# Whole-row first conditioning, head group pairs in sequence, and cached keys spread over the new keys' tiles

## The chip, the cores and the metric

The kernel runs on one core of a Trainium2 chip. The metric is device time in microseconds (us) of one execution; less is better. The core has five engines that each run their own instructions in order: TensorE (PE, with its weight loads PEld), VectorE (DVE), ScalarE (ACT), GpSimd (POOL) and SyncE (SP), which here issues nearly all DMAs.

## The reference

It is one inference step of a two layer encoder over 1024 prompt rows and 32 sample rows of width 1024, all in float32. Layer 0 mixes with an mLSTM, layer 1 with chunk-band attention; each is followed by an MLP.

```
for l in (0, 1):
    sh1, sc1, g1, sh2, sc2, g2 = split(silu(c) @ w_ada[l] + b_ada[l], 6)
    u = x * (1 + sc1) + sh1
    if l == 0:                                  # mLSTM
        q|k, v, o, gates = split(u @ w_in)      # q, k through a causal convolution
        y = (head_norm(mlstm_scan(q, k, v, gates)) * sigmoid(o)) @ w_out
    else:                                       # chunk-band attention
        kv = (x * (1 + kv_scale) + kv_shift) @ w_kv        # one K/V, 4 kv heads
        # 16 heads; a chunk of 64 queries sees its own and the 8 chunks before it;
        # the sample's rows see 512 cached keys and their own 32
        y = softmax(q @ k.T / 8 + bias) @ v @ w_out
    x = layer_norm(alpha * x + (1 + g1) * y)
    u = x * (1 + sc2) + sh2
    x = layer_norm(alpha * x + (1 + g2) * (square(relu(u @ w_up)) @ w_down))
```

The conditioning vector c differs between prompt and sample rows. The outputs are the last x of both, and the new states and K/V rows.

## The kernel before

Every product of full precision is made of three matmuls on a high and a low half (`proj`, lines 118 to 120, and the v steps at 455 to 457): high by high, high by low, low by high. Weights arrive in a `raw` tile and are split into halves of a `wc` tile, the high one by an ACT cast (L89), the low one by a DVE subtraction (L90); `wtile` does both. The pool `ring` has 3 slots for `raw` and 6 for `wc`; a slot is used again when its last reader is done. The 1056 rows are cut into three blocks `TBS`: 384, 384 and 288.

A work list, `Flow`, holds generators with due times. The main loops call `flow.tick()`, and a generator that is due puts its next instructions in there; `finish` puts in what is left. A scheduler then orders each engine's instructions, except for PE in the attention, whose order is kept as written.

The places that the change touches, in order of time:

**The start.** `ada_start(half)` (L386) makes the first conditioning (shift and scale of layer 0) in two halves. Each half takes, for each of 8 chunks of c, two blocks of 128 x 512 of `w_ada` (256 KB) through tiles that rotate over several tags, and adds into two groups of 32 PSUM partitions (`ada`, L392). The sums are copied to `sada` (L399), transposed (L401) and the bias is added (L403). Half 0 gives chunks 0 to 3 of the modulation: then the first four chunks of the v projection of head 0 (`v_proj`, `first_half`) run for three row tiles, while half 1 is loaded. `x_block` (L367) transposes x chunk by chunk into PSUM (L375), modulates it from there (`modulate`: ACT L324, DVE L326 and L329) into `U`, high and low, and copies it to `xt` (ACT, L380), from which it is written to DRAM (`xsp`) for the residual. A v tile is 8 chunks of 3 matmuls. Behind v_0 come the q and k projections (`qk`) and the recurrences.

**Keys and values.** Four tiles of cached keys are split (`kd_c`, ACT L1135, DVE L1136) and transposed (`kt_c`, PE L1141, in `put_keys`) one after another; then comes a loop over nine tiles of new rows, each with 48 matmuls against `wkv`.

**Attention.** `att_group(gp, c, e)` is one chunk c (16 is the sample) of one kv head, 2 gp + e: scores `s` (PE, L1234), bias and row maximum `mx` (DVE, L1245), exponential (ACT, L1248), transposition of `p` (`pt`, L1264) to `pT`, and the value product `pv` (L1284), whose result is split in place into `QO`. A list alternates wide and slim chunks, and takes gp 0 and gp 1 of a chunk next to each other. The bias rows lie in four `wc` tiles (bias0 to bias3) throughout.

**The junction.** After attention `open_acc(1, fwd)` loads the residual's three blocks (`acc<-xsp`, L808), `gain_shift` (ACT, L893) scales them, 24 instructions, and `out_proj` (L962) runs the output projection `op_b` in two groups of column pairs, (0,) and (1, 2, 3), over the blocks 2, 1, 0. `wo_block` loads and casts its weights (`w_ob`) when a group begins.

**The norm of layer 1.** `norm` is a generator: sums, then after `w[0]` ticks a mean (`mean_n`), then after `w[1]` ticks a variance (`var_n`, both PE, L842), then the modulated input `u` of the MLP. For the first norm of layer 1 the delays are `W10`, and a tick is worth 4 or 3 for each projected tile. Before a block's first `up` matmuls its norm is finished.

Of the kernel before, what the change touches and what calls it, by code (L numbers as in the profile page):

```python
# [15 lines left out]
P = 128  # L16
# [59 lines left out]
def trunk_kernel(ctx: ExitStack, tc: tile.TileContext, a, o):  # L76
# [120 lines left out]
    PRE = 3  # L197
    pre = {(k, q): ada_load(k, q, wc_tile) for k, q in ((0, 0), (0, 2), (1, 0), (1, 2))[:PRE]}
    c_rows = raw_tile([16, P], "c_rows")
    nc.sync.dma_start(c_rows[0:8], a["c_prompt"].rearrange("b (k p) -> (b k) p", p=P))  # L200
    nc.sync.dma_start(c_rows[8:16], a["c_sample"].rearrange("b (k p) -> (b k) p", p=P))
    tp = tpt("tp_c")
# [13 lines left out]
    rows2 = raw_tile([NPT2, P], "rows2")  # L216
    nc.sync.dma_start(rows2[0:96], a["b_ada"].rearrange("l (k p) -> (l k) p", p=P))
    nc.sync.dma_start(rows2[96:112], a["b_ada_kv"].rearrange("(k p) -> k p", p=P))
# [112 lines left out]
    START = 5  # L331
# [18 lines left out]
    def rot(fs):  # L350
        seq = [f for f, n in fs for _ in range(n)]
        cnt = [0]

        def f(shape, name):
            cnt[0] += 1
            return seq[cnt[0] % len(seq)](shape, name)
        return f

# [8 lines left out]
    def x_block(t0, n, load=True):  # L367
        if load:
            x_load(t0, n)
        for k in range(KC):  # L370
            ps = tpt(f"xps_{t0}_{k}")
            for i in range(0, n, P):
                xr = xrows[t0, i]
                m = xr.shape[0]
                nc.tensor.transpose(ps[:, i:i + m], xr[:, k * P:(k + 1) * P], ident[:m, :m])  # L375
# [4 lines left out]
            nc.scalar.copy(xt[:, k, t0:t0 + n], ps[:, :n])  # L380
            yield
        nc.sync.dma_start(xsp[0][:, :, t0:t0 + n], xt[:, :, t0:t0 + n])

    start_tile = rot([(raw_tile, 3), (wc_tile, 4), (y_tile, 1), (rc_tile, 1)])

    def ada_start(half):  # L386

        ps = adat(f"ada_0{half}")
        for k in range(KC):
            for q in (half, half + 2):  # L390
                raw = pre.pop((k, q), None) or ada_load(k, q, start_tile)
                nc.tensor.matmul(ps[32 * q:32 * q + 32, :512], cs[:, k, :], raw[:, :512],  # L392
                                 start=(k == 0), stop=(k == KC - 1))
            yield
        sb = rc_tile([P, 512], f"sada_0{half}")
        ps2 = nmt(f"adat_0{half}")
        for i, q in enumerate((half, half + 2)):
            rows = slice(32 * q, 32 * q + 32)
            (nc.scalar.copy if i else nc.vector.tensor_copy)(sb[rows], ps[rows, :512])  # L399
            for b in range(4):  # L400
                nc.tensor.transpose(ps2[:, i * P + b * 32:i * P + b * 32 + 32], sb[rows, b * P:(b + 1) * P],  # L401
                                    ident[rows, rows])
            nc.vector.tensor_tensor(  # L403
                ada[:, 4 * q:4 * q + 4, :], ps2[:, i * P:(i + 1) * P].rearrange("p (b j) -> p b j", b=4)[:, :, 0:2],
                pt2[:, 4 * q:4 * q + 4][:, :, None].broadcast_to([P, 4, 2]), op=ALU.add)
        ap = ada[:, KC + 4 * half:KC + 4 * half + 4, :]
        nc.vector.tensor_scalar_add(ap, ap, 1.0)

    ag = flow.add(ada_start(0))
    for i in range(START):  # L410
        flow.tick()
    x_load(*TBS[0])
    flow.finish(ag)
    xg = [x_block(t0, n, t0 == TBS[2][0]) for t0, n in TBS]


# [20 lines left out]
    def v_proj(h, after, first=None):  # L437
        ncols = 264 if h == 0 else 256

        def srcs(r0):  # L440
            def f(raw):
                r = [(raw[:, :, 0:256],
                      w_in[r0:r0 + 512, 1024 + h * 256:1024 + (h + 1) * 256].rearrange("(k p) c -> p k c", p=P))]
                if h == 0:
                    r.append((raw[:, :, 256:264], w_in[r0:r0 + 512, 3072:3080].rearrange("(k p) c -> p k c", p=P)))
                return r
            return f
        ws = [wtile(f"v{h}_0", srcs(0), ncols)]
        vts = []

        def part(ps, t, ks):
            for k in ks:
                w = ws[k // 4]
                uh, ul = uap(0, k, t * P, P), uap(1, k, t * P, P)
                nc.tensor.matmul(ps[:, :ncols], uh, w[:, 0, k % 4, :], start=(k == 0), stop=False)
                nc.tensor.matmul(ps[:, :ncols], uh, w[:, 1, k % 4, :], start=False, stop=False)
                nc.tensor.matmul(ps[:, :ncols], ul, w[:, 0, k % 4, :], start=False, stop=(k == KC - 1))
        begun, between = first(part) if first else ([], None)
        ws.append(wtile(f"v{h}_1", srcs(512), ncols, between=between))
        for t in range(NT):  # L460
            m = P if t < NT - 1 else TS
            if t < len(begun):
                ps = begun[t]
                part(ps, t, range(4, KC))
            else:
                ps = mmt(f"v_{h}_{t}")
                part(ps, t, range(KC))
            vt = A.tile([P, 258], F32, tag="vt", name=f"vt_{h}_{t}", bufs=9)
            nc.scalar.copy(vt[:m, :256], ps[:m, :256])
            nc.gpsimd.memset(vt[:m, 256:258], 1.0)  # L470
            if h == 0:
                nc.vector.tensor_copy(bass.AP(g64.tensor, g64[:m, t, 0:4].offset, [g64[:m].ap[0], [32, 2], [1, 4]]),
                                      ps[:m, 256:264].rearrange("p (a b) -> p a b", a=2))
            vts.append(vt)
            after(t)
        return vts
# [220 lines left out]
    xa = [None, None, xg[2]]  # L697

    def after_v0(t):
        flow.tick()  # L700
        if t == 2:
            flow.finish(xa[1])
            flow.add(xa[2])
        elif t == 5:
            flow.finish(xa[2])
    def first_half(part):

        ag = flow.add(ada_start(1))
        for _ in range(4):
            next(xg[0])  # L710
            flow.tick()
        begun = []
        for t in range(TBS[0][1] // P):
            begun.append(mmt(f"v_0_{t}"))
            part(begun[t], t, range(4))
            flow.tick()
        flow.finish(ag)

        def rest():
            x_load(*TBS[1], wc_tile)  # L720
            for _ in xg[0]:
                pass
            xa[1] = flow.add(xg[1])
            flow.add(small_params(), SP)
        return begun, rest
    vts = [v_proj(0, after_v0, first_half)]
# [89 lines left out]
    W10 = (8.0, 8.0, 0.0, 0.0, 0.0, 3.0)  # L816
# [355 lines left out]
    for t in range(4):  # L1172
        cr = tmp_t([P, 256], f"ck_{t}")
        nc.sync.dma_start(cr, ck[t * P:(t + 1) * P])
        flow.add(put_keys(cr, P, TP + t * P, f"c{t}"))
        flow.tick()
# [140 lines left out]
    pts = {}  # L1317

    wide = [(gp, c) for c in (8, 12, 13, 14, 15, 9, 10, 11) for gp in range(2)]
    slim = [(gp, c) for c in (7, 6, 5, 4, 16, 3, 2, 1, 0) for gp in range(2)]  # L1320
    units = []
    for i in range(18):
        units += wide[i:i + 1] + slim[i:i + 1]
    with tc.manual_schedule(engines={mybir.EngineType.PE}):
        for gp, c in units:
            for e in range(2):
                flow.add(att_group(gp, c, e))
                flow.tick()
# [6 lines left out]
    accs_cm, acc = open_acc(1, fwd)  # L1335
# [13 lines left out]
    wo = a["w_out_b"][0]  # L1349

    def wo_block(pr, half):
        cols = wo[:, 256 * pr:256 * pr + 256]
# [81 lines left out]
```

## Time and profile before

| | us |
|---|---|
| median of 3 runs | 2532.17 (2531.4 to 2533.92) |
| profiled execution | 2531.46 |
| span of its profile | 2529.6 |
| PE busy | 2466.1 (97%) |
| DVE busy | 1677.0 (66%) |
| ACT busy | 953.2 (38%) |
| POOL busy | 165.8 (7%) |
| bytes moved by DMA | 201.20 MB, 80 GB/s on average |

The profile has busy times by engine, a chain that ended last (followed back from the last instruction), waits by releaser, windows with the clock that the throttle granted to PE, and a timeline. A line such as `PE op_b L118 <- ACT w_ob L89: 6.4, 2, 5.0` says that PE waited at line 118 for the tile w_ob of ACT's line 89, 6.4 us over 2 times, the longest 5.0. A timeline line starts with the start and the duration, names engine, line, operation, the tile written and the tiles read, and ends with the idle time before it and what ended that. Consecutive matmuls overlap in these records, so a matmul's cost in a stream is the distance between two starts.

### The profile page before, as it was taken

How to read it: one execution, taken by the hardware profiler on the slowest of the kernel's cores; microseconds unless marked ns; L12 is line 12 of the kernel's file. 1: busy time of each engine (PE TensorE's matmuls, PEld its weight loads, DVE VectorE, ACT ScalarE, POOL GpSimd, SP SyncE). 2: the span in 40 equal slices, each digit the busy share in tenths (PEclk: the TensorE clock that was granted, in tenths of full speed). 3: DMA queues.
4: the chain of work that ended last, by engine and by line, in shares of the span. 5: the costliest groups of instructions: out<-in, count | busy, mean ns of one | idle time of the engine just before them, and what ended most of it. 6: DMA issues, size and time to landing. Idle time of an engine off the chain costs nothing.

```text
span 2529.6 us, 39897 instructions
## 1 busy us (share of the span) xinstructions
PE 2466.1 (97%) x15784; PEld 2356.0 (93%) x15784; DVE 1677.0 (66%) x3851; ACT 953.2 (38%) x2023; POOL 165.8 (7%) x315
## 2 busy tenths in 40 slices
PE   7999999999999999999999899989999999999998
PEld 3899999999999999999999877689999999999997
DVE  3899998788678678766597677737634334343337
ACT  3654446383212211221376566637621221221222
POOL 0111100000000000000001144400000000000003
PEclk9999999999999999999999999989999999999999
DMA  7522323413224234223123400051111111111101
GB/s 235 166 89 92 95 80 105 152 34 102 90 85 136 81 94 132 87 90 122 59 84 102 101 1 1 6 156 34 51 51 42 51 43 50 42 59 34 51 26 70
DMA packets 192063, 201.20 MB, mean 80 GB/s; under 512 B 9336, under 2 KB 180748, under 8 KB 191876
## 3 DMA queue, kind: packets, MB, share of 16 engines
q1 hardware_dynamic: 191876, 198.65, 25.4%
q8 instruction: 124, 2.03, 0.3%
q14 instruction: 63, 0.52, 0.1%
HBM read 183.38 MB, written 17.60 MB: 79 GB/s over the span
## 4 chain that ended last, share of the span: by engine, by line
PE 83%; DVE 7%; ACT 3%; DMA 3%; issue 1%; SPq 0%; DVEq 0%; POOL 0%; ACTq 0%
PE dn L118 10%; PE dn L120 10%; PE dn L119 10%; PE up L118 10%; PE up L119 9%; PE up L120 9%; PE pv L1284 2%; PE pt L1264 2%; PE s L1234 2%; DVE ada_room L236 1%; PE q L118 1%; PE q L119 1%; PE q L120 1%; DMA ada_room<-in_w_ada_dram 1%; PE op_a L118 1%; PE op_a L119 1%
## 5 line engine op out<-in xcount | busy, mean ns | idle before, releaser
L118 PE MATMUL dn<-h,w_dn 128*128 128x384 f32 (+2 forms) x1568 | 505.9, 323 | 0.0
L120 PE MATMUL dn<-h,w_dn 128*128 128x384 f32 (+2 forms) x1568 | 502.1, 320 | 0.0
L119 PE MATMUL dn<-h,w_dn 128*128 128x384 f32 (+2 forms) x1568 | 497.8, 317 | 0.0
L959 DVE SCALAR_TENSOR_TENSOR acc<-dn,ada,acc 128x384 f32<-128x384 f32 (+5 forms) x536 | 244.0, 476 | 237.2 <-PE dn L120 235.0
L118 PEld LDWEIGHTS dn<-h,w_dn 128*128 128x128 f32 x1568 | 294.5, 188 | 0.8 <-issue 0.2
L119 PEld LDWEIGHTS dn<-h,w_dn 128*128 128x128 f32 x1568 | 294.3, 188 | 0.1
L120 PEld LDWEIGHTS dn<-h,w_dn 128*128 128x128 f32 x1568 | 294.0, 187 | 0.0
L998 DVE TENSOR_TENSOR r<-r 128x384 f32<-128x384 f32 (+1 forms) x192 | 100.0, 523 | 275.6 <-ACT h L997 275.0
L996 ACT ACTIVATE r<-up 128x384 f32<-128x384 f32 (+1 forms) x192 | 88.5, 462 | 448.0 <-PE up L120 437.2
L118 PE MATMUL up<-U,w_up 128*128 128x384 f32 (+1 forms) x768 | 249.3, 325 | 0.0
L119 PE MATMUL up<-U,w_up 128*128 128x384 f32 (+1 forms) x768 | 248.2, 323 | 0.0
L120 PE MATMUL up<-U,w_up 128*128 128x384 f32 (+1 forms) x768 | 247.4, 322 | 0.0
L118 PE MATMUL up<-u,w_up 128*128 128x384 f32 (+1 forms) x768 | 246.5, 321 | 0.0
L120 PE MATMUL up<-u,w_up 128*128 128x384 f32 (+1 forms) x768 | 246.5, 321 | 0.0
L119 PE MATMUL up<-u,w_up 128*128 128x384 f32 (+1 forms) x768 | 246.4, 321 | 0.0
L89 ACT CAST w_up<-raw_up 128x1024 fp32r<-128x1024 f32 x64 | 66.8, 1048 | 413.1 <-PE dn L120 274.3
L236 DVE SCALAR_TENSOR_TENSOR aacc<-rada,cs,aacc 128x256 f32<-128x256 f32 x448 | 190.4, 478 | 0.0
L118 PEld LDWEIGHTS up<-U,w_up 128*128 128x128 f32 x768 | 144.2, 188 | 0.1
L120 PEld LDWEIGHTS up<-U,w_up 128*128 128x128 f32 x768 | 144.3, 188 | 0.0
L120 PEld LDWEIGHTS up<-u,w_up 128*128 128x128 f32 x768 | 144.2, 188 | 0.0
L119 PEld LDWEIGHTS up<-U,w_up 128*128 128x128 f32 x768 | 144.2, 188 | 0.0
L119 PEld LDWEIGHTS up<-u,w_up 128*128 128x128 f32 x768 | 144.1, 188 | 0.0
(318 smaller groups left out, 5260.5 us busy)
## 6 DMA issues: line engine op xcount, KB each, us to landing
raw_up<-in_w_up_dram SPq DMA_DIRECT2D x64, 512.0 KB
raw_dn<-in_w_down_dram SPq DMA_DIRECT2D x64, 512.0 KB
rada<-in_w_ada_dram SPq DMA_DIRECT2D x48, 512.0 KB
ada_room<-in_w_ada_dram SPq DMA_DIRECT2D x32, 512.0 KB
rada<-in_w_ada_dram SPq DMA_DIRECT2D x32, 256.0 KB
rada<-in_w_ada_kv_dram SPq DMA_DIRECT2D x16, 512.0 KB
acc<-xsp SPq DMA_DIRECT2D x4, 1536.0 KB
rc<-rc_d SPq DMA_DIRECT2D x8, 528.0 KB
```

Of the source, the lines that this page charges most:

```text
L89: nc.scalar.copy(dst_h, src)
L118: nc.tensor.matmul(ps, wh, mov(0, k), start=(k == 0), stop=False)
L119: nc.tensor.matmul(ps, wh, mov(1, k), start=False, stop=False)
L120: nc.tensor.matmul(ps, wl, mov(0, k), start=False, stop=(k == nk - 1))
L236: nc.vector.scalar_tensor_tensor(acc[:, cnd], raw[:, k], sc, acc[:, cnd], op0=ALU.mult, op1=ALU.add)
L959: nc.vector.scalar_tensor_tensor(xs, ps[:, off + o:off + o + mm_], gate[:, fc, cnd:cnd + 1], xs, op0=ALU.mult, op1=ALU.add)
L996: nc.scalar.activation(r, ps[:, :n], AF.Relu)
L998: nc.vector.tensor_mul(r, r, r)
L1234: nc.tensor.matmul(s[:, b, :w], qst, kk[i][:, g, k0 + j0:k0 + j0 + w], start=(i == 0), stop=(i == 1))
L1264: nc.tensor.transpose(pt[:kp, j - j0, pr * P:(pr + 1) * P], ps_[pr][:, j * P:j * P + kp], ident)
L1284: nc.tensor.matmul(pv[64 * e:64 * e + 64, :nq], V[:kp, vt0 + j, g * 64:(g + 1) * 64], pts[e][:kp, j, :nq], start=(j == 0), stop=(j == nt - 1))
```

## The change

Four things are changed together.

1. **Start.** `ada_load(k)` loads a whole row block of `w_ada`, 128 x 2048, as two DMAs of 512 KB into one `wc` tile; `c_rows` and the bias rows are loaded ahead of them. On SP's queue follow rows 0 to 3, x block 0, rows 4 and 5, half of the v weights, rows 6 and 7, the other half, x blocks 1 and 2. `ada_mm(k)` adds four products into four groups of 32 partitions, and `ada_first` transposes once for all; the 1 of 1 + scale is added to the bias beforehand. x is transposed to `xt` first (`x_transpose`) and modulated from there (`u_chunks`). v of head 0 (`v_first`) runs block by block and, within a block, chunk by chunk over three tiles; between chunks stand the transposes and the modulation of the next block. The writes to `xsp` stand behind v.
2. **Cached keys.** `cached_keys(t)` becomes a generator on the work list, started at the new tiles 0, 2, 4 and 6.
3. **Attention and output projection.** All 17 chunks of gp 0 come before those of gp 1. In gp 1, after units 8 and 11, the two halves of the first output projection weight are loaded and cast in `wc` slots of bias tiles that no later unit reads. `open_acc` loads the blocks in the order in which they are used (2, 1, 0), with the weight pairs 1 and 2 between them.
4. **Norm delays.** `W10` begins with 10, 12 instead of 8, 8.

The diff, without removed helpers:

```
-    def ada_load(k, q, mk):
-        raw = mk([P, 512], f"rada_0_{k}_{q}")
-        nc.sync.dma_start(raw, a["w_ada"][0, k * P:(k + 1) * P, q * 512:(q + 1) * 512])
+    def ada_load(k):
+        raw = wc_tile([P, 2 * D], f"rada_0_{k}")
+        for i in range(2):
+            nc.sync.dma_start(raw[:, i * D:(i + 1) * D], a["w_ada"][0, k * P:(k + 1) * P, i * D:(i + 1) * D])
         return raw
...
+    adaw = [ada_load(k) for k in range(4)]
...
+    nc.vector.tensor_scalar_add(pt2[:, KC:2 * KC], pt2[:, KC:2 * KC], 1.0)
...
+    def x_transpose(t0, n, eng):
+        for k in range(KC):
+            ps = tpt(f"xps_{t0}_{k}")
...
+            eng[k % len(eng)](xt[:, k, t0:t0 + n], ps[:, :n])
+            yield
+    def u_chunks(t0, n):
+        for k in range(KC):
             for off, m, cnd in segs(t0, n):
                 tmp = A.tile([P, 384], F32, tag="tmp", name=f"utmp_{t0}_{k}_{off}", bufs=3)
-                modulate(ps[:, off:off + m], m, sc1[:, k, cnd:cnd + 1], sh1[:, k, cnd:cnd + 1],
+                modulate(xt[:, k, t0 + off:t0 + off + m], m, sc1[:, k, cnd:cnd + 1], sh1[:, k, cnd:cnd + 1],
                          uap(0, k, t0 + off, m), uap(1, k, t0 + off, m), tmp[:, :m])
             yield
+    def ada_mm(k):
+        for q in range(4):
+            nc.tensor.matmul(ada_ps[32 * q:32 * q + 32, :512], cs[:, k, :], adaw[k][:, q * 512:(q + 1) * 512],
+                             start=(k == 0), stop=(k == KC - 1))
+    def ada_first():
+        sb = rc_tile([P, 512], "sada")
+        ps2 = nmt("adat")
+        for hf in range(2):
+            (nc.scalar.copy if hf else nc.vector.tensor_copy)(sb[:, 256 * hf:256 * hf + 256],
+                                                              ada_ps[:, 256 * hf:256 * hf + 256])
+            for b in (2 * hf, 2 * hf + 1):
+                nc.tensor.transpose(ps2[:, b * P:(b + 1) * P], sb[:, b * P:(b + 1) * P], ident)
...
+    def v_first(ws, nxt):
+        vts = []
+        for bi, (t0, n) in enumerate(TBS):
+            ts = range(t0 // P, (t0 + n + P - 1) // P)
+            pss = {t: (mmt, nmt, mmt)[bi % 2 * (t % 2)](f"v_0_{t}") for t in ts}
+            for k in range(KC):
+                for t in ts:
+                    v_chunk(pss[t], ws, t, k)
+                nxt(bi, k)
+            vts += [v_out(pss[t], 0, t) for t in ts]
         return vts
...
+    xT = [x_transpose(t0, n, (nc.scalar.copy, nc.vector.tensor_copy)[:2 - (i > 0)]) for i, (t0, n) in enumerate(TBS)]
+    uT = [u_chunks(t0, n) for t0, n in TBS]
+    x_load(*TBS[0])
+    adaw += [ada_load(k) for k in (4, 5)]
+    for k in range(4):
+        ada_mm(k)
+    vw = [v_weight(0, 0)]
+    adaw += [ada_load(k) for k in (6, 7)]
+    for k in range(4, 6):
+        ada_mm(k)
+    for _ in xT[0]:
+        pass
+    for k in range(6, 8):
+        ada_mm(k)
+    vw.append(v_weight(0, 1))
+    x_load(*TBS[1], wc_tile)
+    x_load(*TBS[2])
+    ada_first()
+    for _ in uT[0]:
+        pass
+    flow.add(small_params(), SP)
...
+    vts = [v_first(vw, next_u)]
+    for t0, n in TBS:
+        nc.sync.dma_start(xsp[0][:, :, t0:t0 + n], xt[:, :, t0:t0 + n])
...
-    def open_acc(l, order):
+    def open_acc(l, order, between=None):
...
-        for ti in order:
+        for ti in order if between is None else reversed(order):
             t0, n = TBS[ti]
             nc.sync.dma_start(accs[ti], xsp[l][:, :, t0:t0 + n])
+            if between:
+                between(ti)
...
-    W10 = (8.0, 8.0, 0.0, 0.0, 0.0, 3.0)
+    W10 = (10.0, 12.0, 0.0, 0.0, 0.0, 3.0)
...
-    for t in range(4):
+    def cached_keys(t):
         cr = tmp_t([P, 256], f"ck_{t}")
         nc.sync.dma_start(cr, ck[t * P:(t + 1) * P])
-        flow.add(put_keys(cr, P, TP + t * P, f"c{t}"))
-        flow.tick()
         nc.sync.dma_start(V[:, 8 + t], cv[t * P:(t + 1) * P])
+        yield 3.0
+        yield from put_keys(cr, P, TP + t * P, f"c{t}")
     for t in range(NT):
+        if t % 2 == 0 and t < 8:
+            flow.add(cached_keys(t // 2))
...
-    wide = [(gp, c) for c in (8, 12, 13, 14, 15, 9, 10, 11) for gp in range(2)]
-    slim = [(gp, c) for c in (7, 6, 5, 4, 16, 3, 2, 1, 0) for gp in range(2)]
-    units = []
-    for i in range(18):
-        units += wide[i:i + 1] + slim[i:i + 1]
+    wide, slim = (8, 12, 13, 14, 15, 9, 10, 11), ((7, 6, 5, 4, 16, 3, 2, 1, 0), (16, 7, 6, 5, 4, 3, 2, 1, 0))
     with tc.manual_schedule(engines={mybir.EngineType.PE}):
-        for gp, c in units:
-            for e in range(2):
-                flow.add(att_group(gp, c, e))
-                flow.tick()
+        for gp in range(2):
+            for i in range(17):
+                c = slim[gp][i // 2] if i % 2 else wide[i // 2] if i < 16 else slim[gp][8]
+                for e in range(2):
+                    flow.add(att_group(gp, c, e))
+                    flow.tick()
+                if gp and i in (8, 11):
+                    wo_pre[0, len(wo_pre)] = wo_block(0, len(wo_pre))
...
-    accs_cm, acc = open_acc(1, fwd)
+    def more_wo(ti):
+        if ti:
+            for half in range(2):
+                wo_pre[3 - ti, half] = wo_block(3 - ti, half)
+    accs_cm, acc = open_acc(1, fwd, more_wo)
...
+    def wo_get(pr, half):
+        return wo_pre.pop((pr, half), None) or wo_block(pr, half)
...
-    out_proj([(0,), (1, 2, 3)], rev, wo_block, o_mov, ada_part(1, 2), end_out1, "b", width=[384, 384, 320])
+    out_proj([(0,), (1, 2, 3)], rev, wo_get, o_mov, ada_part(1, 2), end_out1, "b", width=[384, 384, 320])
```

More of the change, by code (lines that the diff above doesn't have):

```diff
@@ L348, in rc_tile @@
         return A.tile(shape, F32, tag="rc", name=name, bufs=1)
[L350 to L357, printed above, removed]
     def x_load(t0, n, mk=y4_tile):
@@ L379, in x_block @@
                          uap(0, k, t0 + off, m), uap(1, k, t0 + off, m), tmp[:, :m])
-            nc.scalar.copy(xt[:, k, t0:t0 + n], ps[:, :n])
             yield
[L382 to L407, printed above, removed]
@@ L409, in trunk_kernel @@
-    ag = flow.add(ada_start(0))
-    for i in range(START):
-        flow.tick()
-    x_load(*TBS[0])
-    flow.finish(ag)
-    xg = [x_block(t0, n, t0 == TBS[2][0]) for t0, n in TBS]
+    ada_ps = adat("ada_0")
+    def ada_mm(k):
[10 more added lines that the diff above has]
+                nc.tensor.transpose(ps2[:, b * P:(b + 1) * P], sb[:, b * P:(b + 1) * P], ident)
+        nc.vector.tensor_tensor(
+            ada[:, 0:16, :].rearrange("p (q b) j -> p q b j", q=4),
+            ps2.rearrange("p (b q j) -> p q b j", b=4, q=4)[:, :, :, 0:2],
+            pt2[:, 0:16].rearrange("p (q b) -> p q b", q=4)[:, :, :, None].broadcast_to([P, 4, 4, 2]), op=ALU.add)
@@ L435, in trunk_kernel @@
     cst = {}
[L437 to L448, printed above, removed]
-        vts = []
[L451 to L459, printed above, removed]
-        for t in range(NT):
[L461 to L474, printed above, removed]
-            after(t)
@@ new lines, in v_weight, with srcs, v_chunk @@
+    def v_weight(h, half):
+        def srcs(raw):
+            r0 = 512 * half
+            r = [(raw[:, :, 0:256],
+                  w_in[r0:r0 + 512, 1024 + h * 256:1024 + (h + 1) * 256].rearrange("(k p) c -> p k c", p=P))]
+            if h == 0:
+                r.append((raw[:, :, 256:264], w_in[r0:r0 + 512, 3072:3080].rearrange("(k p) c -> p k c", p=P)))
+            return r
+        return wtile(f"v{h}_{half}", srcs, 264 if h == 0 else 256)
+    def v_chunk(ps, ws, t, k):
+        w = ws[k // 4]
+        n = w.shape[-1]
+        uh, ul = uap(0, k, t * P, P), uap(1, k, t * P, P)
+        nc.tensor.matmul(ps[:, :n], uh, w[:, 0, k % 4, :], start=(k == 0), stop=False)
+        nc.tensor.matmul(ps[:, :n], uh, w[:, 1, k % 4, :], start=False, stop=False)
+        nc.tensor.matmul(ps[:, :n], ul, w[:, 0, k % 4, :], start=False, stop=(k == KC - 1))
@@ new lines, in v_out, with v_proj @@
+    def v_out(ps, h, t):
+        m = P if t < NT - 1 else TS
+        vt = A.tile([P, 258], F32, tag="vt", name=f"vt_{h}_{t}", bufs=9)
+        nc.scalar.copy(vt[:m, :256], ps[:m, :256])
+        nc.gpsimd.memset(vt[:m, 256:258], 1.0)
+        if h == 0:
+            nc.vector.tensor_copy(bass.AP(g64.tensor, g64[:m, t, 0:4].offset, [g64[:m].ap[0], [32, 2], [1, 4]]),
+                                  ps[:m, 256:264].rearrange("p (a b) -> p a b", a=2))
+        return vt
+    def v_proj(h, after):
+        ws = [v_weight(h, half) for half in range(2)]
+        vts = []
+        for t in range(NT):
+            ps = mmt(f"v_{h}_{t}")
+            for k in range(KC):
+                v_chunk(ps, ws, t, k)
+            vts.append(v_out(ps, h, t))
+            after(t)
+        return vts
@@ L695, in tick, with next_u @@
         flow.tick()
-    xa = [None, None, xg[2]]
-    def after_v0(t):
-        flow.tick()
[L701 to L710, printed above, removed]
-            flow.tick()
[L712 to L726, printed above, removed]
+    xT = [x_transpose(t0, n, (nc.scalar.copy, nc.vector.tensor_copy)[:2 - (i > 0)]) for i, (t0, n) in enumerate(TBS)]
[19 more added lines that the diff above has]
+    flow.add(small_params(), SP)
+    def next_u(bi, k):
+        if bi < 2:
+            next(xT[bi + 1])
+            next(uT[bi + 1])
+            if k == KC - 1:
+                for g in (xT[bi + 1], uT[bi + 1]):
+                    for _ in g:
+                        pass
+        flow.tick()
+    vts = [v_first(vw, next_u)]
+    for t0, n in TBS:
+        nc.sync.dma_start(xsp[0][:, :, t0:t0 + n], xt[:, :, t0:t0 + n])
     flow.finish()
@@ L1317, in trunk_kernel, with wo_block @@
     pts = {}
[L1319 to L1328 removed]
+    wo = a["w_out_b"][0]
+    wo_pre = {}
+    def wo_block(pr, half):
+        cols = wo[:, 256 * pr:256 * pr + 256]
+        return wtile(f"ob{pr}_{half}", lambda raw: [
+            (raw[64 * e:64 * e + 64], cols[(2 * half + e) * 256:(2 * half + e + 1) * 256].rearrange(
+                "(r d) c -> d r c", d=64)) for e in range(2)])
+    wide, slim = (8, 12, 13, 14, 15, 9, 10, 11), ((7, 6, 5, 4, 16, 3, 2, 1, 0), (16, 7, 6, 5, 4, 3, 2, 1, 0))
+    with tc.manual_schedule(engines={mybir.EngineType.PE}):
+        for gp in range(2):
[6 more added lines that the diff above has]
+                    wo_pre[0, len(wo_pre)] = wo_block(0, len(wo_pre))
         flow.finish()
```

19 lines of the change are left out of this document (3 added, 16 removed).

## The prediction

> **What bounds the kernel now.** I read the page first (busy shares, then the chain that ended last), then the waits of TensorE over the whole span, and then windows and timelines of the places where those waits lie.
>
> ```profile
> PE 2466.1 (97%) x15784; PEld 2356.0 (93%) x15784; DVE 1677.0 (66%) x3851; ACT 953.2 (38%) x2023; POOL 165.8 (7%) x315
> ...
> PE 83%; DVE 7%; ACT 3%; DMA 3%; issue 1%; SPq 0%; DVEq 0%; POOL 0%; ACTq 0%
> ```
>
> TensorE (PE) is busy 2466.1 of 2529.6 us and holds 83% of the chain. The change hardly alters how many matmuls there are, so it can only recover PE time that is waited away or run at a lower clock. The waits say how much there is; the columns are engine, line, releaser: total us, times, longest.
>
> ```profile
> PE s L1234 <- DVE mx L1245: 7.2, 15, 3.0
> PE op_b L118 <- ACT w_ob L89: 6.4, 2, 5.0
> PE var_n L842 <- ACT qr_n L89: 2.9, 2, 2.0
> PE xps L375 <- ACT xt L380: 2.9, 2, 2.4
> PE kt_c L1141 <- DVE kd_c L1136: 1.8, 2, 1.3
> PE kt_c L1141 <- ACT kd_c L1135: 1.4, 2, 1.0
> PE mean_n L842 <- ACT sr_n L89: 1.2, 1, 1.2
> ```
>
> These fall in four places: the start (xps), the cached keys (kt_c), attention (s) with the junction behind it (op_b), and the layer 1 norm (mean_n, var_n). The change touches all four. A measurement of this kernel can tell about 0.2%, 5 us, from no change.
>
> **1. The start.** Columns: stretch and length; busy (count) of PE, weight loads, DVE, ACT and POOL; granted clock; DMA share; GB/s.
>
> ```profile
> 20.00:30.00 10.00, 6.46 (x26) 2.49 (x25) 4.55 (x9) 4.04 (x7) 0.00 (x0) 0.84 0.88 282
> 40.00:50.00 10.00, 7.20 (x35) 2.73 (x33) 1.71 (x5) 1.81 (x3) 0.23 (x5) 1.00 0.35 97
> 50.00:60.00 10.00, 9.21 (x61) 8.47 (x61) 7.94 (x17) 7.75 (x17) 0.00 (x0) 0.83 0.53 195
> ```
>
> PE is booked as busy for 6.46 and 7.20 us of two 10 us stretches before 50, on 26 and 35 instructions against 61 afterwards: conditioning matmuls waiting for their rows. DVE and ACT do little there. The timeline and the transfers of the first 45 us show the rest (start, duration; the GB/s row has 40 buckets of 1.125 us):
>
> ```profile
> 21.45 0.68 DVE L399 COPY sada<-ada 32x512 f32<-32x512 f32 x1 [14.05 <-PE ada L392]
> 24.72 0.64 PE L455 MATMUL v<-w_v,U 128*128 128x264 f32 x3 [1.35 <-ACT U L324]
> 43.61 2.76 PE L392 MATMUL ada<-rada,cs 128*32 128x512 f32 x10
> 50.72 0.90 PE L375 MATMUL xps<-ident,xr 128*128 128x128 f32 x3 [2.39 <-ACT xt L380]
> 53.40 0.67 ACT L324 ACTIVATE U<-xps,ada 128x384 fp32r<-128x384 f32 x1 [0.80 <-PE xps L375]
> 53.60 0.42 PE L455 MATMUL v<-w_v,U 128*128 128x264 f32 x1
> 53.82 0.42 PE L456 MATMUL v<-w_v,U 128*128 128x264 f32 x1
> 54.81 0.48 ACT L380 COPY xt<-xps 128x384 f32<-128x384 f32 x1 [0.38 <-DVE utmp L326]
> 56.01 0.28 PE L456 MATMUL v<-w_v,U 128*128 128x264 f32 x1
> 56.13 0.28 PE L457 MATMUL v<-w_v,U 128*128 128x264 f32 x1
> 86.62 0.42 PE L118 MATMUL qk<-U,w_qk 128*128 128x384 f32 x1
> GB/s 0 75 335 319 176 348 228 239 300 373 411 401 422 399 399 379 331 73 232 327 357 58 311 291 304 337 401 341 129 320 290 215 111 300 333 11 0 0 0 0
> DMA packets 6417, 11.11 MB, mean 247 GB/s; under 512 B 1168, under 2 KB 1808, under 8 KB 6416
> ```
>
> Before, the last conditioning matmul ends at 46.4 and the first qk starts at 86.6, because most of v_0 waits for the second half of the conditioning. The change puts the v steps behind all the conditioning but lets them follow one another.
>
> Bytes ahead of the last row: 8 rows x 1.05 MB, x block 0 (1.57 MB), the v weights (1.1 MB) and 0.06 MB, 11.1 MB in all, as many as before moved in 45 us. The buckets show 373 to 422 GB/s where transfers stand queued, and dips to 58 to 240 where the loads wait for a slot. Now the first four rows and x have slots of their own, and the later rows wait only for slots of rows that PE has long read. I take 375 GB/s: 29.6 us. Before, the flow began at some 2.2 (second and third bucket); four small loads now go ahead of the rows, so I let it begin at 3.5, and the last row lands at 33. From the copy of the accumulator (21.45) to the first v (24.72) took 3.3 us before; four matmuls of 0.28 (2.76/10) come ahead, less what the copy saves, now split between two engines: first v at 37.
>
> One v matmul takes 0.12 us (56.01 to 56.13); a chunk is 9 of them, 1.09, and beside 16 of the 24 chunks stand three transposes of the next block (0.25: the 0.90 of 50.72 is at the low clock, 0.45 without it, and its last end overlaps what follows). 24 x 1.09 + 16 x 0.25 = 30.2. Beside each of the 16, ACT owes one U (0.67) and one copy of transposed x (0.48), 1.15 against PE's 1.34; so PE leads narrowly, and I add 2.3 us of waits. While PE's queue stands on rows its clock may fall: matmuls at 53.60 and 53.82 stand 0.22 apart, 0.12 warm; 20 such are 2 us. End 37 + 30.2 + 2.3 + 2 = 71.5, against 86.6: **-15** (-19 with no waits and a full clock; -10 with ACT in the lead). The write-backs of xt go behind the v stage's loads on SP's queue, two of them ahead of the qk weights; the second waits for block 1's copies, done some 11 us into v, which leaves 20 us for the 3 MB and the first weights: no cost, and if that cover went, a first-weight wait of some 2 us. DVE's next full stretch lies past 100 us, where PE idles:
>
> ```profile
> 100.00:110.00 10.00, 7.61 (x45) 7.23 (x45) 9.91 (x14) 2.83 (x4) 4.99 (x4) 0.94 0.02 3
> ```
>
> There DVE bounds, and before 50 us it was nearly free, so it starts its work earlier by the same 15 us and the shift survives.
>
> [...]
>
> **2. Cached keys.** The two kt_c rows, 1.8 + 1.4 = 3.2 us, are PE waiting for casts, with nothing else to run. Spread over tiles 0, 2, 4 and 6 of the new keys, they find PE at work. DVE is the cover that can go: in this stretch it has 9.26 of 10 us already.
>
> ```profile
> 1390.00:1400.00 10.00, 8.40 (x69) 7.92 (x68) 9.26 (x17) 6.87 (x16) 0.36 (x1) 1.00 0.22 55
> ```
>
> **-3** (-4 with PE refilled, +1 if DVE's casts are late for a new key tile).
>
> **3. Attention.** Order gp 0 then gp 1: the bias rows of heads 8 to 15 are needed 17 chunks later.
>
> ```profile
> 1448.96 0.76 DVE L1245 CUSTOM_DVE_ANT_0 p<-s,bias 128x576 f32<-128x576 f32 x1 [1.80 <-DMA bias<-bias_d]
> ```
>
> DVE stood 1.80 us for a bias, and the longest wait for mx was 3.0: **-2** (-5 to 0). In the middle 34 units stay 34 units; two weight halves are cast there, 1.05 us on ACT and 1.23 on DVE each (rows below), on engines with room: 0 (-2 to +3).
>
> **4. The junction.** The columns of the op_b row are those of the windows; the GB/s row covers 1640 to 1680, 1 us a bucket.
>
> ```profile
> 1646.00:1682.00 36.00, 28.77 (x148) 28.21 (x149) 3.50 (x8) 0.83 0.89 229
> 1647.12 1.05 ACT L89 CAST w_ob<-raw_ob 128x1024 fp32r<-128x1024 f32 x1
> 1648.20 1.23 DVE L90 TENSOR_TENSOR w_ob<-raw_ob,w_ob 128x1024 fp32r<-128x1024 f32 x1 [0.52 <-ACT w_ob L89]
> 1648.22 0.64 PE L118 MATMUL op_b<-QO,w_ob 128*128 128x320 f32 x1 [1.41 <-ACT w_ob L89]
> 1652.14 13.85 ACT L893 ACTIVATE acc<-acc,pt 128x384 f32<-128x384 f32 x24 [3.97 <-DMA acc<-xsp]
> 1653.17 0.31 PE L118 MATMUL op_b<-QO,w_ob 128*128 128x320 f32 x1
> 1653.32 0.31 PE L119 MATMUL op_b<-QO,w_ob 128*128 128x320 f32 x1
> 1656.16 0.34 PE L119 MATMUL op_b<-QO,w_ob 128*128 128x384 f32 x1
> 1656.34 0.34 PE L120 MATMUL op_b<-QO,w_ob 128*128 128x384 f32 x1
> 1666.97 0.63 PE L118 MATMUL op_b<-QO,w_ob 128*128 128x320 f32 x1 [5.01 <-ACT w_ob L89]
> 1681.26 0.34 PE L120 MATMUL op_b<-QO,w_ob 128*128 128x384 f32 x1
> GB/s 0 0 0 232 224 206 218 223 370 378 373 373 372 372 373 368 359 355 355 202 219 213 222 208 190 16 0 0 0 39 307 208 221 216 205 214 162 17 182 239
> ```
>
> The first weight of the projection is cast only after the last value product (1.41 us). The second one stands on ACT behind 24 scalings of acc (13.85 us), which wait for 4.15 MB of acc (370 GB/s, from 1648 on) ahead of it, so PE stands 5.01 us and then restarts at the lower clock (0.83 mean).
>
> Group 0 has 144 matmuls: 48 of 320 columns at 0.15 and 96 of 384 at 0.175 are 24.0 us. It ran from 1648.22 to 1681.4, 33.2 us; with the 1.41 ahead the loss is 10.6, and the last four value products lose about 1 more to the thin end of attention. With group 0's two halves loaded and cast inside gp 1 all this goes, if ACT and DVE have them done by then; acc and the group 1 weights then arrive behind 24 us of PE work: 4.15 MB / 370 = 11 us and four halves of 0.5 MB at 215 GB/s, 10 us, are 21 for what group 1 needs first. That is close, and what would be late next are ACT's scalings and those casts: I take **-9.5** (-6 to -11.9).
>
> **5. Norm delays.** Mean after 10 ticks instead of 8, variance after 12. The two waits above hold 2.9 + 1.2 = 4.1 us, the most that can be gained. Each later step also delays the conditioned input of the next up matmuls by one up tile, 24 x 0.175 = 4.2 us, of which I take 3 as hidden behind the other blocks' work, as the var_n waits of 2.9 in all suggest that the tiles before were short of such cover by about that: 4.1 gained, 2.6 given back by waits for u. **-1.5** (-4 to +5).
>
> **Sum.** -15 - 3 - 2 + 0 - 9.5 - 1.5 = -31. The profiled execution took 2531.46 (span 2529.6 and 1.86 around it), so 2500.5; the median of the three runs is 0.71 above the profiled one: **2501 us**.
>
> **The rivals.** (a) The start gives nothing (0.15). If the rows come at the mean of the first 45 us, 247 GB/s, 11.1 MB take 45 us, the first v starts at 3.5 + 45 + 4 = 52.5 and v ends at 87, so no gain; 2516. For: that mean is what the same queue gave over 45 us. Against: its dips are slot waits, which the change shortens.
> (b) The norm gives back the junction (0.12). If ACT's casts and scalings of acc 0, now loaded last, hold the third tile's norm, PE waits the 5 at step 5 instead of gaining 1.5; 2507.5.
> (c) The weights for the projection don't get ahead (0.06): the slots of the bias tiles become free later than unit 11 of gp 1, the casts stand in ACT's queue in front of pT copies, or the last half of group 1 is late by the same 5 us. The junction keeps its 5.01 wait and half of its cold part: -3 instead of -9.5; 2507.5.
> (d) Other side (0.06): slower than before. The place is attention, 34 units (2 gp x 17 chunks) up to 1648.22. With one gp at a time, neighbours in PE's order no longer share a chunk, and in gp 1 ACT and DVE, both in order, hold the pT copies behind weight casts whose loads (0.5 MB at 215 GB/s, 2.4 us) are under way; if PE's s then waits for mx in every unit, it decides from 31/34 = 0.9 us a unit on. At 1.2 us the stage loses 41 us: 2542. For: those waits exist (7.2 us over 15). Against: they come to 0.2 us a unit, and only two casts are added.
>
> [...]
>
> **How the numbers follow.** Forecast 0.61, (a) 0.15, (b) 0.12, (c) 0.06, (d) 0.06. Ends: with the good bounds of steps 1, 4 and 5 together the time is 2501 - 4 - 2.4 - 2.5 = 2492; some of the attention's ends go below that: 2488. Upward, (a) at 2516 with 2 us of the attention's bound above it is 2518. About 0.1 lies on each side. Faster by over 0.2%: all but (d) and a corner in which (a), (b) and (c) meet: 0.91; within 0.2%: 0.03; slower: 0.06.
>
> **What would show it.** In the profile after: the first v matmul at 37 us and the first qk at 71.5; rates of 370 and more through the first 30 us; no kt_c rows among PE's waits; op_b directly behind the last pv, with neither of its two waits, and its mean clock over 0.95 in group 0; var_n and mean_n waits under 1 us, with no wait of up for u in their place. Wrong it would be if the first v came after 45 us, if waits for mx were over 20 us, or if PE waited for the last half of w_ob.

## The result, and the profile after

The changed kernel took 2515.53 us (median of 4 runs, 2509.76 to 2518.4) against 2531.78 of the kernel before on the same chips: ratio 0.9933, interval 0.9913 to 0.9954. That is 16.3 us faster. The forecast was 31 us. Of its five steps, two gave about what was forecast, two gave nothing that the runs show, and one cost time; a further loss lay where nothing had been forecast.

Busy times of the page after, and PE's waits over the whole span (engine, line, releaser: total us, times, longest):

```profile
PE 2459.1 (98%) x15772; PEld 2357.2 (94%) x15772; DVE 1666.9 (66%) x3850; ACT 949.3 (38%) x2018; POOL 166.8 (7%) x315
...
PE s L1239 <- DVE mx L1250: 5.8, 13, 2.0
PE ada L383 <- DMA rada<-in_w_ada_dram: 5.8, 9, 2.2
PE kv L1192 <- DVE uk L90: 3.4, 2, 3.0
...
PE var_n L844 <- ACT qr_n L89: 2.0, 1, 2.0
```

The waits for kd_c and w_ob are gone. In their place stands a wait of `kv` for uk, 3.4 us, that the kernel before did not have.

The start, as the timeline and the transfers of the first 45 us show it (in the GB/s row, 40 buckets of 1.125 us):

```profile
33.29 1.05 PE L383 MATMUL ada<-rada,cs 128*32 128x512 f32 x4 [0.23 <-DMA rada<-in_w_ada_dram]
36.79 0.39 PE L435 MATMUL v<-w_v,U 128*128 128x264 f32 x1 [0.86 <-ACT U L326]
71.93 0.42 PE L118 MATMUL qk<-U,w_qk 128*128 128x384 f32 x1
GB/s 0 7 51 197 339 390 408 390 397 339 411 371 422 419 408 419 430 422 415 408 400 355 280 338 350 408 408 411 408 408 408 415 408 408 312 38 5 0 11 374
DMA packets 6319, 14.38 MB, mean 320 GB/s; under 512 B 1640, under 2 KB 3214, under 8 KB 6318
```

First v at 36.79 (forecast 37), first qk at 71.93 (forecast 71.5). From 4.5 to 23.6 us the transfers run at 339 to 430 GB/s without the dips of before; from there to 28 us they fall to between 280 and 355.

The junction:

```profile
1637.96 1.17 PE L1289 MATMUL pv<-pT,V 64*64 64x256 f32 x4
1639.06 0.41 PE L118 MATMUL op_b<-QO,w_ob 128*128 128x320 f32 x1
1640.00:1650.00 10.00, 10.00 (x59) 10.00 (x58) 3.55 (x6) 5.25 (x9) 0.00 (x0) 0.86 0.98 297
1650.00:1660.00 10.00, 10.00 (x59) 10.00 (x59) 3.78 (x5) 7.81 (x12) 0.00 (x0) 1.00 1.11 287
1660.00:1670.00 10.00, 10.00 (x66) 10.00 (x65) 3.01 (x5) 6.79 (x10) 0.00 (x0) 1.00 0.66 138
```

op_b follows the last value product with no idle time, and in the windows (columns as in the prediction) PE is never idle; only the first 10 us are at 0.86 of the clock.

The starts of the first and last timeline rows of each stage cut both traces into pieces (the last `pv` row holds four matmuls). All times are us:

| piece | before | after | difference | forecast |
|---|---|---|---|---|
| start to first `up` of layer 0 | 531.59 | 518.93 | -12.7 | -15 |
| from there to first `s` (keys and values lie in it) | 910.02 | 911.86 | +1.8 | -3 |
| first `s` to last `pv` | 203.57 | 207.17 | +3.6 | -2 |
| last `pv` to first `dn` of layer 1 (junction and norm) | 174.00 | 162.58 | -11.4 | -11 |
| first `dn` of layer 1 to first `yt` | 650.11 | 653.56 | +3.5 | 0 |

The pieces add up to -15.2. Another 0.3 us is lost behind the first `yt`, and -14.9 is the difference of the two spans. The last row is the surprise: in this piece PE has no wait at all in either trace, and the instructions are the same.

### The profile page after: what moved, and what is told of

It is laid out like the page before. It is cut to its first block, busy times and chain, and to the rows that moved or that the text cites. A ratio compares the mean times of both kernels' runs of the same rounds, so it can differ in the third digit from the quotient of the medians.

```text
span 2514.8 us, 39869 instructions
## 1 busy us (share of the span) xinstructions
PE 2459.1 (98%) x15772; PEld 2357.2 (94%) x15772; DVE 1666.9 (66%) x3850; ACT 949.3 (38%) x2018; POOL 166.8 (7%) x315
## 4 chain that ended last, share of the span: by engine, by line
PE 84%; DVE 5%; ACT 3%; DMA 3%; issue 1%; POOL 0%; SPq 0%; DVEq 0%; POOLq 0%; ACTq 0%
PE dn L119 10%; PE dn L118 10%; PE dn L120 10%; PE up L118 9%; PE up L120 9%; PE up L119 9%; PE pv L1289 2%; PE pt L1269 2%; PE s L1239 2%; DMA ada_room<-in_w_ada_dram 1%; PE o L118 1%; PE q L118 1%; PE o L119 1%; PE o L120 1%; PE q L119 1%; PE q L120 1%
```

## The experiments

Ratios are to the kernel before, run on the same chip.

| label | what | median us | ratio, interval |
|---|---|---|---|
| e1 | start only | 2523.64 | 0.9966, 0.9952 to 0.9979 |
| e2 | all without the spread keys | 2509.67 | 0.9915, 0.9901 to 0.9928 |
| e3 | all with delays 8, 8 | 2513.82 | 0.9930, 0.9917 to 0.9942 |
| e4 | attention and junction only | 2519.72 | 0.9959, 0.9946 to 0.9971 |
| e5 | e2 and an unused wc tile first | 2505.55 | 0.9898, 0.9884 to 0.9911 |
| e6 | e2 and two unused raw tiles first | 2512.59 | 0.9924, 0.9911 to 0.9938 |
| e7 | all, keys at tiles 0 to 3 | 2513.14 | 0.9925, 0.9912 to 0.9937 |
| e8 | spread keys only | 2534.74 | 1.0010, 1.0001 to 1.0019 |
| e9, e10, e11 | e2 and 2, 3, 6 unused wc tiles | 2507.17, 2507.59, 2505.03 | one run each |
| e12 | e7, one unused wc tile, addition on POOL | 2506.08 | 0.9900, 0.9884 to 0.9917 |

**e1, the start alone.** All hunks of the diff up to the writes of `xsp`, nothing else.

> Only the start of the change, all else as before. Theory A (read from the changed trace): the first qk starts 14.7 us earlier, the chain of gate rows behind v gives 2 us back, and 12.5 us are left at the end: ratio 0.995. Rival B (the prediction's step 1): the shift survives the recurrence, 15 us left: ratio 0.994. Rival C: the time lost in the last MLP (92.9 us instead of 92.46 for each group of up and down products) comes with the start, by another order of slots: then 9 us are left, and the pace is 92.9 here.

The start's own gain is there: first qk at 71.79, first `up` 15.4 us earlier. But only 7.5 us were left in the median and 9.4 at the end of its trace. From the first `dn` of layer 1 to the first `yt` this kernel took 653.58 us, as the whole change did. So rival C was right: the slow last MLP comes with the start. It is 3.5 of the 6.0 us lost; the rest is scattered over the stages between, in one trace.

**e2, the cached keys ahead again.**

```
-    def cached_keys(t):
+    for t in range(4):
         cr = tmp_t([P, 256], f"ck_{t}")
         ...
+        flow.add(put_keys(cr, P, TP + t * P, f"c{t}"))
```

> The whole change without the spreading of the cached keys: they stand ahead of the new keys again. Theory A: the cached keys had covered the late third and fourth tiles of x, so the wait of 3.4 us for uk goes and the two waits for kd_c of 3.2 us come back; the attention's ramp, which now starts behind the copies of the last cached tile and with a cold clock, gets 2 us back: 1 to 3 us faster than the whole change, some 2513. Rival B (the prediction): the spreading is worth 3 us, so 3 us slower, 2518.5.

Its median was 5.9 us below that of the whole change, which was run apart from it, and 4.2 below that of e3, which ran beside it and differs from it only by the spreading and the delays. Both are more than theory A had said, and the slowest execution of e2 (2511.85) is faster than the fastest of e3 (2512.34). Attention took 202.49 us instead of 207.17. Spreading was a loss.

**e3, the old delays.**

```
-    W10 = (10.0, 12.0, 0.0, 0.0, 0.0, 3.0)
+    W10 = (8.0, 8.0, 0.0, 0.0, 0.0, 3.0)
```

> The whole change with the old norm delays, 8 and 8. Theory A: the delays were worth 2.4 us between the junction and the first down products, so 2.4 us slower than the whole change. Rival B (the prediction's rival b): the later variance holds the up products back (it has 2.0 and 0.9 us of waits there), so 2 to 4 us faster than the whole change. Rival C: the slower last MLP (92.9 us a group) comes from the delays: then the pace here is 92.46.

From the first op_b to the first `dn` it took 161.33 us, the whole change 161.48. Neither theory is borne out: no gain and no loss from the delays is seen. But the nine kernels with the new delays and the new junction took from 159.84 to 163.54 us here, so a gain as small as 1.5 us isn't excluded. The waits of the two kernels from 1636 to 1802 us, e3 first, change in number and length:

```profile
PE var_n L844 <- ACT qr_n L89: 3.1, 2, 2.0
PE mean_n L844 <- ACT sr_n L89: 1.7, 1, 1.7
```

```profile
PE mean_n L844 <- ACT sr_n L89: 0.9, 1, 0.9
...
PE up L120 <- DVE w_up L90: 0.5, 1, 0.5
```

With the 2.0 of var_n above, the whole change has 3.4 us of these waits and e3 4.8; the sum of the piece doesn't show it. The executions overlap (2512.34 to 2515.81, and 2509.76 to 2518.4).

**e4, attention and junction alone.** The hunks on `open_acc`, the unit order, `wo_pre` and `wo_get`.

> Only the order of attention, the early projection weights and the order of acc; start, cached keys and delays as before. Theory A: the junction gives 9 us, attention's middle loses 1, its ramp is as before, so 7 to 8 us faster than before: 2524. Rival B: the order of attention itself costs the 3.6 us that the changed trace lost there, so 5.4 us faster: 2526.4. Rival C: the pace of the last MLP goes with this part (92.9 us a group), and only 4 us are left.

11.5 us faster than before, better than either theory. The last `pv` row to the first op_b fell from 3.04 to 1.10 us, first op_b to first `dn` from 170.96 to 160.98. Attention took 203.77 against 203.57: its order shows neither a cost nor a gain. The last MLP took 650.11, as before.

**e5, e6: the slots.** e2 with, ahead of `c_rows`,

```
+    pad = wc_tile([P, 8], "pad_wc")
+    nc.gpsimd.memset(pad, 0.0)
```

or two such tiles by `raw_tile`.

> The change without the spread cached keys (as in the second experiment), and one unused small tile of the tag wc ahead of all others, so that every later wc tile lies in the slot in which it lay before (the new start takes 8 of these tiles where the old took 9, of 6 slots). Theory A: the up products of layer 1, 8.44 us for 48 matmuls of 384 columns with the new start and 8.33 with the old, depend on which slot their weights lie in: 8.33 here, 3.5 us less than 2509.7, some 2506. Rival B: they depend on the slot of the raw tiles, or on nothing that slots decide: 8.44, and the same time.

> The change without the spread cached keys, and two unused small tiles of the tag raw ahead of all others (the new start takes 2 raw tiles where the old took 7, of 3 slots), so that raw tiles lie in their old slots. Theory A (the wc slot decides): 8.44 us for 48 up matmuls, same time, 2509.7. Rival B (the raw slot decides): 8.33 us, some 2506.

The unused wc tile took 4.1 us off the median and 3.46 off the last MLP (650.10); the raw tiles took nothing off it (653.55). The first `up` and the next `dn` of one group in layer 1, in the trace after, then in that of e5:

```profile
1846.94 0.29 PE L118 MATMUL up<-u,w_up 128*128 128x288 f32 x1
1893.50 0.29 PE L118 MATMUL dn<-h,w_dn 128*128 128x288 f32 x1
```

```profile
1842.17 0.29 PE L118 MATMUL up<-u,w_up 128*128 128x288 f32 x1
1888.23 0.30 PE L118 MATMUL dn<-h,w_dn 128*128 128x288 f32 x1
```

The same 288 matmuls take 46.56 us in the one and 46.06 in the other (46.05 before). The `dn` products of layer 1 take 46.40 us a group in both; in layer 0 the groups differ by some hundredths.

**e8, the spreading alone**, on the kernel before.

> Only the spreading of the cached keys, all else as before. Theory A: PE waits for uk behind DVE's queue (3 us), and attention's ramp is 4 us longer: 4 to 6 us slower than before, ratio 1.002. Rival B (the prediction's step 2): 3 us faster, ratio 0.999.

2.4 us slower (2534.74 against 2532.3), so the sign of step 2 was wrong on its own ground too, though by less than theory A had it. From the first `q` to the first `s` it gained 0.9 us, and attention took 205.97 instead of 203.57.

**e7, spread earlier.**

```
-        if t % 2 == 0 and t < 8:
-            flow.add(cached_keys(t // 2))
+        if t < 4:
+            flow.add(cached_keys(t))
```

> The whole change, with the cached keys started at new tiles 0, 1, 2 and 3 instead of 0, 2, 4 and 6. Theory A: of what the spreading costs, one part (4.7 us in attention) comes from the last cached tile, whose key copies end just when attention starts, so that PE runs its ramp at half clock; here they end earlier and attention takes 203 us from first score to last value product instead of 207.2. The other part, 1.2 to 4 us in the key stage, stays: some 2512. Rival B: attention's 4.7 us come from its own order or from chance: 207 again, 2515.5.

Attention took 203.55 us, as with the keys ahead. By the same cut e3, which spreads as the whole change does, took 207.2. So the 3.6 us go with the last cached tile at attention's door. It is the stage that shows it: the median, 2513.14, is 2.4 us below that of the whole change, and the executions overlap. The windows from 1430 to 1450 us, in which attention begins, for the whole change, e2 and e7:

```profile
1430.00:1450.00 20.00, 14.74 (x69) 11.40 (x69) 12.14 (x39) 9.91 (x27) 5.68 (x8) 0.66 0.62 138
```

```profile
1430.00:1450.00 20.00, 15.19 (x106) 11.71 (x105) 14.09 (x46) 11.55 (x31) 7.54 (x14) 1.00 0.62 139
```

```profile
1430.00:1450.00 20.00, 16.33 (x98) 12.57 (x97) 13.04 (x43) 11.04 (x29) 7.42 (x12) 0.83 0.63 139
```

Attention begins at 1430.8, 1430.8 and 1430.7 us. PE is busy for 14.7 to 16.3 us each time, but with 69 instructions at a granted 0.66, 106 at 1.00 and 98 at 0.83. The clock alone does not decide this: e8, whose attention begins at 1440.7 us, has e7's clock, 0.83, and yet only 68 instructions in its first 20 us:

```profile
1441.00:1461.00 20.00, 13.42 (x68) 10.24 (x67) 11.47 (x39) 9.85 (x25) 6.07 (x9) 0.83 0.61 133
```

What the kernels with a late cached tile share is DVE's work as attention begins. These are rows of the whole change, then of e2:

```profile
1430.34 2.69 DVE L1148 CAST k<-kt_n 64x256 fp32r<-64x256 f32 x8
1433.06 0.76 DVE L1250 CUSTOM_DVE_ANT_0 p<-s,bias 128x576 f32<-128x576 f32 x1
```

```profile
1429.22 1.73 DVE L1148 CAST k<-kt_n 64x256 fp32r<-64x256 f32 x4 [1.17 <-ACT k L1148]
```

In the whole change DVE is copying eight key blocks when attention begins, PE's second group of scores waits 0.5 us for one of them, and the first row maximum starts 2.3 us after the first `s` (2.0 in e2); e3 and e8 show the same wait, and no other kernel does. From the first `s` to the first `pv` these three took 18.28, 18.25 and 18.62 us at clocks of 0.66, 0.83 and 0.83 in the first 20 us; the kernel before took 15.99, and the other ten 13.51 to 15.08 at 0.83 to 1.00. So the loss stands when the first value product starts. How the late copies grow to some 3 us on the way there was not tested.

**e9, e10, e11: two, three and six unused wc tiles.**

> As the kernel with one unused wc tile, but with two: every wc tile lies one slot further on than in the kernel before. Theory A (what counts is whether the two halves of an up weight lie in slots 0-1, 2-3, 4-5 or in 1-2, 3-4, 5-0): 8.44 us for 48 up matmuls of 384 columns in layer 1, as without a tile. Theory B (what counts is one slot or its neighbours in memory): another value, 8.33 or between.

> With three unused wc tiles: an even number of slots away from the kernel before. Theory A (even or odd): 8.33 us for 48 up matmuls. Theory B (the slot itself): another value than with two.

> The change without the spread cached keys, with six unused wc tiles, a full turn of the six slots: every later wc tile lies where it lay without any. Theory A (the slot decides): 8.44 us for 48 up matmuls of 384 columns in layer 1, and 3.5 us more from the first down product on than with one, two or three tiles. Rival B (it is the unused tile as such, by its instruction or its place in the program, that makes the difference): 8.33.

The last MLP took 650.10, 650.10 and 650.11 us: fast each time. Theory A of e9 and e10 (even or odd slots) and that of e11 (the slot) both fell. The kernel with six tiles has the slot turn of none and yet is fast. Nor is it the unused tile as such, e11's rival B: the kernel before, e4 and e8 have none and are fast, and e6 has two of the other tag and is slow. What is left is which tag is used first. The old start and the wc pads take a wc tile first; the new start and the raw pads take a raw tile first. All eight kernels with wc ahead (before, e4, e5, e8 to e12) took 650.10 to 650.11 us in this piece, all six with raw ahead (after, e1, e2, e3, e6, e7) 653.55 to 653.58. That is a full agreement, seen after the runs. One reading is that the pool lays its tags out in the order in which they are first used. Then all wc tiles lie higher by the three raw slots, 12,672 bytes of each partition (the widest raw tile has 4 x 264 floats). The profiles hold no addresses, so this is not shown; why the `up` products of layer 1 should run 1% slower, and no others, stays open too.

**e12, the addition on POOL**, with e7 and one unused wc tile.

```
-        nc.vector.tensor_add(x, x, kvsh[:, :, cnd:cnd + 1].broadcast_to([P, KC, m]))
+        nc.gpsimd.tensor_add(x, x, kvsh[:, :, cnd:cnd + 1].broadcast_to([P, KC, m]))
```

> The whole change with the cached keys started at new tiles 0 to 3, one unused wc tile, and the addition of the shift to x moved from DVE to POOL. Theory A: PE waited for uk in the key stage because DVE, in order, stood on that addition until POOL and a late transfer were done, with the low half of an earlier uk behind it; on POOL the addition blocks nobody, the wait of 3 us for uk goes, and the spreading gives some 2 to 3 us after all: 2503 against 2505.6 with the cached keys ahead. Rival B: uk is late by its transfer or its slot itself: the wait stays, 2506 or more.

The reason for it are these rows of the whole change:

```profile
1386.17 1.90 POOL L1168 TENSOR_TENSOR x<-x,kvss 128x1024 f32<-128x1024 f32 x1 [7.97 <-DMA x<-xsp]
1388.10 1.23 DVE L1169 TENSOR_TENSOR x<-x,kvss 128x1024 f32<-128x1024 f32 x1 [5.43 <-POOL x L1168]
1389.24 1.22 DVE L90 TENSOR_TENSOR uk<-x,uk 128x1024 fp32r<-128x1024 f32 x1
1390.52 0.58 PE L1192 MATMUL kv<-w_kv,uk 128*128 128x256 f32 x1 [3.00 <-DVE uk L90]
```

POOL waits 7.97 us for a late tile of x, DVE 5.43 for POOL, and PE 3.00 for the low half that DVE makes next. In e12 the wait for uk was 0.4 us, but one of `kt_n` for kd_n came up:

```profile
PE kt_n L1145 <- DVE kd_n L1140: 3.0, 2, 2.0
...
PE kv L1194 <- DVE uk L90: 0.4, 1, 0.4
```

Its 2506.08 are not better than the 2505.55 of e5. And since e7 without the move had only 0.9 us of waits for uk, e12 doesn't prove the reading; it shows that the key stage has another wait ready. The same holds of all variants: PE's waits in the key stage are 3.2 us in the kernel before and 4.0 in e2, all for cached keys, and with spreading 3.4 (whole change), 4.3 (e3), 3.9 (e7), 2.3 (e8) and 3.4 (e12), mostly for other tiles. That DVE stood on the addition is read from the rows, not shown by an experiment.

## Why the prediction was right, and where it was off

The time lay in the range and on the side that was forecast, at about half the size.

- **Step 1, the start: right in time, partly by luck.** First v, first qk and the last row (its matmuls start at 33.29, 33 was forecast) came within half a microsecond. The rates did not quite: 370 GB/s and more was asked for through the first 30 us, and from 23.6 to 28 us they were 280 to 355. From first v to first qk it took 35.1 us, 34.5 was forecast, but with other terms. PE had no idle time in it and the granted clock was 1.00, so the 2.3 us of waits and the 2 of a low clock were not there; the products and transposes alone took 35.1 instead of 30.2 (one v matmul to the next is 0.13 us, not 0.12, and the transposes of the gates were not in the sum). The two errors cancelled. Of the 14.7 us at the first qk, 12.7, 15.4, 13.3, 16.7 and 13.9 were left at the first `up` of layer 0 in five kernels with the same start code (after, e1, e2, e3, e7), 14.4 on average. "The shift survives" held on average; single executions differ by 4 us. Rival (a) was wrong: loads that stand queued did not keep the mean of before, 247 GB/s.
- **Step 2, the cached keys: the step that failed.** -3 was forecast, +1 as the worst. Alone they cost 2.4 us (e8), in the whole change 4.2 (against e3) to 5.9. The step took away 3.2 us of waits for casts and put nothing in their place, with DVE's casts named as the cover that could be gone. Waits of 3.4 us for uk took their place. In the rows, DVE's queue held a low half behind an addition that waited 5.43 us for POOL, which had waited 7.97 for a transfer. And the step didn't look past its own stage: the last cached tile's copies end at attention's door, and there the larger part of the loss lies (2.4 us in e8, 3.6 in the whole change).
- **Step 3, attention: mis-sized.** The -2 for the bias did not come. With the last cached tile out of the way attention took 202.4 to 204.0 us in either order. The +3.6 of the changed trace belongs to step 2. Rival (d) named the right stage, but its mechanism, a cost in each of 34 units, is refuted by e4.
- **Step 4, the junction: right.** -9.5 was forecast; first op_b to first `dn` fell by 10.0 in e4, by 9.5 in the whole change and by 7.4 to 11.1 in all eleven kernels with the new junction, and the gap ahead of op_b by 1.9 us more, 11.4 together with the norm. The mean clock from the first op_b to 1663 us was 0.93, a little under the 0.95 asked for. Neither rival (b) nor rival (c) came.
- **Step 5, the delays: nothing seen instead of -1.5** (161.48 and 161.33). The var_n wait was still 2.0 us, where under 1 was asked for.
- **Not in the prediction:** the 3.5 us of the last MLP, which go with the tag that is used first. The prediction took the work behind the four places to cost the same as before, and no step asked whether the new start changes what a later stage uses.

The sum with what the runs gave: -14.4 for the start, -11.4 for junction and norm, +4.2 for the keys with attention's ramp, +3.5 for the last MLP, 0 for order and delays: -18.1. Measured were 16.3 us between the medians and 14.9 between the two traces; single executions of the changed kernel differ by 8.6 us, so a closer agreement would be luck. That the time lay in the range is luck too: its upper end was set for rival (a), which did not happen, and what filled it were the loss at attention's door, the last MLP, and the gains of steps 2, 3 and 5 that did not come. The best version that ran more than once is e5: the whole change without the spread keys, and the wc tag used first, 2505.55 us, ratio 0.9898.

The 2 us that step 1 put into v for a low clock were an estimate, 20 matmuls at 0.22 us instead of 0.12. PE's waits for rows of `w_ada` ahead of v were 2.2 us at the longest, and in v the clock was 1.00; it was low ahead of v, 0.83 from 20 to 30 us. In the kernel before, the 0.83 from 50 us on stood behind a wait of 2.39 us, and attention's 0.66 in the whole change came with no wait over 2.0. These runs do not show what lowers the clock.

## What to carry to other kernels

A step that removes a wait should be costed with the queue of every engine on which its work is put, and one stage further on, where that work ends. When a stage with no waits becomes slower by the same amount in one group of kernels, look for what that group shares, however far away: here it was which of two pool tags is used first. Undoing one part of a joint change showed here that one of its four parts cost 4 to 6 us of what the others had won.

## What the runs showed of the hardware

Identical streams of matmuls without any wait took 173.5 or 175.8 ns for one of 384 columns (8.33 and 8.44 us for 48) in the `up` products of layer 1, by which tag was used first, with a spread of 0.03 us over 650 us within each group of kernels; those of layer 0 took 8.42 to 8.43 in both. Over the first 20 us of attention the granted clock of PE was 0.66 in the whole change, where its longest wait was 2.0 us, and 1.00 in e2.
